# Heads of 64 dims issued in pairs, and a 64-row logit product padded to 128 rows

## The chip, the cores and the metric

The kernel runs on one core of one Trainium2 chip. The metric is the device time of one execution in microseconds (us). The engines are named as the profile names them: PE is the matrix engine (TensorE), PEld its weight loads, DVE is VectorE, ACT is ScalarE, POOL is GpSimd, and SP issues most of the DMAs. An "fp32r" operand is one that the kernel has rounded so that PE takes it in a single pass; a plain fp32 product is recorded as two passes, that is two matmul records and two weight loads.

## The reference

Two decoder layers (mixer and feed-forward network) and a third block work on 256 tokens of width 1024. Only the attention parts matter here. In short form:

```python
# layer 0, mixer "ab"
o_a = mla_attention(...)          # 8 heads: logits over 96 dims, values of 64 dims
o_b = swa_sink_attention(...)     # 8 heads of 64 dims, 2 key/value heads, a sink per head
# layer 1, mixer "cd"
o_c = forgetting_attention(...)   # 8 heads of 64 dims, decay from running sums of log-sigmoid gates
o_d = chunk_relpos_attention(...) # 8 heads of 64 dims, relative-position bias
# each of them, per head:
logits = q @ k.T * scale + bias   # causal or chunked mask
p = softmax(logits)
o = p @ v                         # 256 tokens x 64 dims
```

The mixers' outputs go through a projection, a residual and a layer norm, then through a SwiGLU network of width 2816. The third block has heads of 128 dims and is not touched by the change.

## The kernel before

Every weight matrix streams in once from one packed array, in blocks of at most 128 x 1032 numbers. A block lands in one of 5 "raw" buffers; ACT rounds it into a high part and DVE subtracts to get the low part (`block`). Both parts are tiles of the pool "h", which has `SLOTS` = 28 buffers and also holds q, k, v, attention outputs (`oT`), and the 11 tiles of the hidden layer (`hid`). The products of activations and weights are three fp32r passes (`gx`, `gw`).

All engine calls are recorded first, in program order, by the class `Order`. It then issues them by a list scheduler with modelled costs: each engine takes the earliest call in program order whose inputs are ready and whose buffer is free. A tile takes its buffer when the first call that touches it is issued. For some kinds of tile `RESERVE` lets a later tile go ahead of earlier ones as long as enough buffers stay free: for "h" a tile that goes ahead must find 4 free ones. Calls without inputs are ready from the start of the schedule; weight loads are paced by the 5 raw buffers, other DMAs by an added dependency (`AHEAD`). The engines then work through the issued order strictly one after the other.

Attention works head by head (`head`): two logit products (query tile 0 against key tile 0, 128 columns; query tile 1 against both, 256 columns) into a PSUM tile `a` of 4; DVE adds the bias and takes the row extreme (`tensor_tensor_reduce`); ACT takes the exponential with row sums; DVE normalises; PE transposes the three 128 x 128 blocks of probabilities; ACT copies them to a tile `pt` of 2; and two value products, plain fp32 with a stationary operand of 64 columns, write 64 of the 128 partitions of `po`. The second head of a pair writes the other 64. `hilo` then splits `po` for the output projection.

Three kinds of logit products occur. The sliding-window heads contract over 64 rows in plain fp32, the two heads of a pair in different halves of the rows. The latent-attention (MLA) heads contract over 96 rows. The "cd" heads use fp32r with the high and low parts of k stacked along the contraction: the first product takes 128 rows, the second one (q's low part `ql` with k's high part) takes 64 rows, in the half that k's high part occupies:

```python
own = slice(g * 64, g * 64 + 64)
self.head([(qq[:, g, i, :], kk[:, g, i, :]), (ql[own, i, :], kk[own, g, i, :])], bias, ...
```

Around the attention, `out_proj` multiplies by the output weights in units of two row tiles (4 "h" buffers each); the last 3 units (4 in the feed-forward network) are held until the end and used for token tile 0 and then for token tile 1, so that the layer norm of tile 0 runs beside the products of tile 1. `ffn` starts with the first 3 column groups (12 "h" buffers) for token tile 0.

Of the kernel before, what the change touches and what calls it, by code (L numbers as in the profile page):

```python
# [28 lines left out]
SLOTS = 28  # L29
# [12 lines left out]
class Order:  # L42
    """Takes the engine calls of the network in program order, and issues them in an order that a list
    scheduler finds: every engine takes the earliest call whose data and whose buffer are there."""
# [18 lines left out]
    def __init__(self, nc):  # L63
        self.ops, self.tiles, self.masks = [], {}, {}
        self.shift, self.pe = 0, []
# [70 lines left out]
    def add(self, eng, real, m, a, k):  # L136
# [3 lines left out]
        o = dict(i=len(self.ops), eng=eng, call=(real, m, a, k), deps=set(), tiles=set(), prio=len(self.ops) + self.shift)  # L140
# [21 lines left out]
        o["cost"] = self.cost(eng, m, a, k, ap_out + ap_in)  # L162
# [11 lines left out]
    def issue(self):  # L174
# [52 lines left out]
        while done < len(ops):  # L227
            for e in engs:
# [3 lines left out]
                while ready[e]:  # L232
# [20 lines left out]
                    if e == "ACT":  # L253
                        tab = self.TABLE.get(o["call"][2][2]) if o["call"][1] == "activation" else None
# [32 lines left out]
            if not ev:  # L287
                if done < len(ops):
                    raise RuntimeError("no call can go: " + str({e: [ops[i]["call"][1] for _, i in ready[e][:3]] for e in engs}))
                break  # L290
# [25 lines left out]
        for o in seq:  # L316
            real, m, a, k = o["call"]
            o["out"] = getattr(real, m)(*a, **k)  # L318


class Net:
    """Emits the whole network; `specs` lists the blocks of the packed weight stream in order."""

    def __init__(self, tc, ctx, a):
# [15 lines left out]
        self.ptp = pool("pt", 2)  # L340
# [9 lines left out]
    # ---- allocation helpers  # L350
# [37 lines left out]
    def w(self, name, li, rows, cols, pool=None):  # L388
        """rows: list of k-tiles (128 row indices each); returns per-k [(wh, wl)] APs of [128, len(cols)]."""
# [22 lines left out]
    def gw(self, out, x, w, c0, m=128):  # L412
        """out[cols, tok] = sum_k w_k[128k, cols].T @ x_k[128k, 256tok]"""
# [18 lines left out]
    # ---- activations held transposed  # L432
# [4 lines left out]
    def to_xT(self, src, t, xt):  # L437
        """src [128 tok, 1024] -> hi/lo parts of xT for token tile t; xt(i, half) gives [128, 4, 256]."""
# [9 lines left out]
    def bcast(self, name, n, off=0, tile_=None):  # L448
        """A row of n numbers on every partition."""
# [64 lines left out]
    def head(self, qk, bias, v, out, sign=-1.0, sink=None):  # L514
        """Causal blocks. qk: pairs [d, 256] whose products add up (q scaled, times sign); bias [128, 384] = t0k0 | t1k0 t1k1."""
        nc, V, mm = self.nc, self.nc.vector, self.nc.tensor.matmul
        s = self.pa()
        for i, (q, k) in enumerate(qk):
            mm(s[:, 0:128], q[:, 0:128], k[:, 0:128], start=i == 0, stop=i == len(qk) - 1)
        for i, (q, k) in enumerate(qk):  # L520
            mm(s[:, 128:384], q[:, 128:256], k, start=i == 0, stop=i == len(qk) - 1)
# [16 lines left out]
        pt = self.probs((L, L), exps, rs, nm, sign, [0, 128, 256], es)  # L538
        mm(out, v[0], pt[:, 0:256], start=True, stop=False)
        mm(out[:, 128:256], v[1], pt[:, 256:384], start=False, stop=True)  # L540
# [19 lines left out]
    # ---- the parts  # L560
# [34 lines left out]
    def rope(self, out, x, cos, sin):  # L595
        """x [128, heads, 32] (PSUM), cos / sin [128, heads, 32] with the scale folded in."""
# [9 lines left out]
    def norm_T(self, src, g, n, dst):  # L606
        """rms norm of PSUM src[t] ([128 tok, n]) with gain g, transposed hi/lo into dst [k] -> (hi, lo)."""
# [14 lines left out]
    def mixer_ab(self):  # L622
# [3 lines left out]
        # c_q | v_s  # L626
# [13 lines left out]
        # c_kv | k_r  # L640
# [15 lines left out]
        # k_s, q_s (pair j: heads j and 4 + j)  # L656
# [15 lines left out]
        # sliding-window attention  # L672
        o = []
        for j in range(4):
            if j % 2 == 0:
                oT = self.h([128, 2, 2, S], F32R)
            po = self.pa()
            for g in range(2):
                hh = 4 * g + j
                self.head([(qTs[g * 64:g * 64 + 64, j, :], kTs[g * 64:g * 64 + 64, :])], Bs[:, hh, :],  # L680
                          [vs[:, t, g * 64:g * 64 + 64] for t in range(2)], po[g * 64:g * 64 + 64, 0:256],
                          sink=(sk[:, 1, hh:hh + 1], sk[:, 0, hh:hh + 1]))
# [51 lines left out]
        for j in range(4):  # L734
            if j % 2 == 0:
                oT = self.h([128, 2, 2, S], F32R)
            po = self.pa()
            for g in range(2):
                hh = 2 * j + g
                self.head([(qTm[hh // 4][:, hh % 4, :], kTm[hh // 4][:, hh % 4, :])], mm_,  # L740
                          [vm[:, t, hh * 64:hh * 64 + 64] for t in range(2)], po[g * 64:g * 64 + 64, 0:256])
# [5 lines left out]
    def out_proj(self, name, li, o, krows, last_units, done, last_cols=(0, 512, 1024)):  # L747
        """o @ W; the last units go token tile by token tile, done(t, [(product, columns)]) after each."""
# [82 lines left out]
    def mixer_cd(self):  # L831
# [4 lines left out]
        # v_c | v_f | f in four groups of 258, token tile by token tile  # L836
# [10 lines left out]
        # log sigmoid of the forget gates, running sums, sums as rows  # L847
# [22 lines left out]
        def pair(cq, ck, scale, j):  # L870
            """q and k of heads 2j .. 2j + 3 with the high and low parts stacked along the contraction: per head
            k = [high; low], q = [high; high], and q's low part beside k's high one. Even heads have their high
            parts in the lower 64 partitions, odd heads in the upper."""
            qq, kk = self.h([128, 2, 2, S], F32R), self.h([128, 2, 2, S], F32R)
            ql = self.h([128, 2, S], F32R)
            lo, up = slice(0, 64), slice(64, 128)
            for c0, isq in ((cq, True), (ck, False)):
# [6 lines left out]
                for b, (own, other) in enumerate(((lo, up), (up, lo))):  # L884
# [3 lines left out]
                    V.scalar_tensor_tensor(ql[own] if isq else dst[other, b], pv[own], sc, dst[own, b].bitcast(F32),  # L888
# [3 lines left out]
        def heads(j, fox, v, qq, kk, ql):  # L892
            for i in range(2):
                oT = self.oT
                po = self.pa()
                for g in range(2):
                    hh = 2 * (j + i) + g
                    if fox:
                        pc = self.pa()
                        for t in range(2):  # L900
                            nc.tensor.transpose(pc[:, t * 128:(t + 1) * 128],
                                                cum[:, t, hh:hh + 1].to_broadcast([128, 128]), self.ident)
                        bias = self.lp([128, 384], F32, tag="L")
                        V.scalar_tensor_tensor(bias[:, 0:128], pc[:, 0:128], ncq[:, 0, hh:hh + 1], cm[:, 0:128],
                                               op0=OP.add, op1=OP.add)
                        V.scalar_tensor_tensor(bias[:, 128:384], pc[:, 0:256], ncq[:, 1, hh:hh + 1], cm[:, 128:384],
                                               op0=OP.add, op1=OP.add)
                    else:
                        bias = Bc[:, hh, :]
                    own = slice(g * 64, g * 64 + 64)  # L910
                    self.head([(qq[:, g, i, :], kk[:, g, i, :]), (ql[own, i, :], kk[own, g, i, :])], bias,
                              [v[:, t, hh * 64:hh * 64 + 64] for t in range(2)], po[g * 64:g * 64 + 64, 0:256],
                              sign=-1.0 if fox else 1.0)
# [11 lines left out]
    def mem_prep(self):  # L925
        """The memory comes transposed; its gain goes in with the split, its rms factor after the products."""
# [51 lines left out]
    def block2(self, mk, mv):  # L978
# [7 lines left out]
        # MOBA: groups of two heads (q q k k)  # L986
# [38 lines left out]
        def gated(po, c0, dst, hh):  # L1025
            """dst (hi, lo) <- po * 2 silu(gate)"""
# [23 lines left out]
        # memory attention  # L1050
# [19 lines left out]
        # gMLP  # L1070
# [39 lines left out]
        # gates and branches  # L1110
# [128 lines left out]
def layout(inputs):  # L1239
    """Everything but the weight stream, laid out for the chip."""  # L1240
# [59 lines left out]
```

## Time and profile before

| what | value |
|---|---|
| median of 3 runs | 952.17 us (951.37 to 955.55) |
| span of the profiled execution | 949.4 us |
| what lies around the span, against the median | 2.8 us |
| PE busy | 940.0 us (99%), 6504 matmuls |
| DVE busy | 602.0 us (63%) |
| ACT busy | 487.5 us (51%) |
| POOL busy | 23.9 us (3%) |
| DMA queue of the weights | 54.3% of 16 engines' span |
| mean granted clock of TensorE | 0.997 |

The span runs from the first to the last instruction. A busy share counts a matmul's pipeline until its end, so two matmuls that follow at 0.1 us may both last 0.28 us; what a matmul costs is better read from the start of one to the start of the next. The stages follow each other as: sliding-window and MLA attention from 39 to 92 us, output projection and layer norm to 130, the feed-forward network to about 298, the projections of mixer "cd" to 335, its attention to 421, output projection and layer norm to 451, the second network to about 630, and the third block to the end.

### The profile page before, as it was taken

To read this page: it belongs to the slowest core of one execution; us is meant where nothing else is said; L and a number is where in the kernel's file an instruction comes from. 1 tells how busy PE (TensorE), PEld (TensorE's weight loads), DVE (VectorE), ACT (ScalarE), POOL (GpSimd) and SP (SyncE) were. 2 spreads that over 40 slices of the span, in tenths; PEclk is the share of its full clock that TensorE was granted. 3 is DMA by queue.
4 is the path that set the end of the run, shared out by engine and by line. 5 is a ranking of instruction groups with operands and counts; after the bars stand their busy time and mean duration, and the time that the engine had idled before them with its cause. 6 is when DMAs were issued, how large, how long until landed. Compare 5 with 4: busy or idle time off the path is not lost.

```text
span 949.4 us, 16237 instructions
## 1 busy us (share of the span) xinstructions
PE 940.0 (99%) x6504; PEld 857.2 (90%) x6504; DVE 602.0 (63%) x1064; ACT 487.5 (51%) x839; POOL 23.9 (3%) x32
## 2 busy tenths in 40 slices
PE   8999999999999999999999999999999999999997
PEld 7977899999889988879999998898889999999996
DVE  5777984545548556779545465495448697565553
ACT  6677474444424757546443455254446574445441
POOL 0100100000001000000000000000000000000000
PEclk9999999999999999999999999999999999999999
DMA  9732595556664714345655768266544545665631
GB/s 324 279 138 80 172 328 166 172 162 216 221 207 171 251 60 129 138 133 172 213 172 155 222 234 295 70 197 222 178 155 141 182 161 189 189 189 179 193 118 45
DMA packets 50155, 171.30 MB, mean 180 GB/s; under 512 B 5920, under 2 KB 7456, under 8 KB 49824
## 3 DMA queue, kind: packets, MB, share of 16 engines
q1 hardware_dynamic: 49792, 169.74, 54.3%
q8 instruction: 51, 0.84, 0.3%
q10 hardware_dynamic: 288, 0.52, 0.1%
q14 instruction: 24, 0.20, 0.1%
HBM read 169.19 MB, written 1.05 MB: 179 GB/s over the span
## 4 chain that ended last, share of the span: by engine, by line
PE 96%; DVE 1%; DMA 1%; ACT 1%; POOL 0%; issue 0%; SPq 0%; POOLq 0%; ACTq 0%
PE g L318 85%; PE a L318 10%; DVE h L318 1%; DMA raw<-in_wstream_dram 1%; DMA h<-in_wstream_dram 1%; POOL s L318 0%; ACT h L318 0%; DVE res L318 0%; SPq L318 0%; DVE s L318 0%; DVE xT L318 0%; ACT y L318 0%; POOLq L1294 0%; ACT xT L318 0%; ACT pt L318 0%
## 5 line engine op out<-in xcount | busy, mean ns | idle before, releaser
L318 PE MATMUL g<-h,h 128*128 128x256 f32 (+2 forms) x2520 | 438.2, 330 | 0.0
L318 DVE TENSOR_TENSOR h<-raw,h 128x1024 fp32r<-128x1024 f32 (+4 forms) x300 | 349.4, 1184 | 127.8 <-PE g L318 51.9
L318 PEld LDWEIGHTS g<-h,h 128*128 128x128 f32 x2520 | 371.3, 188 | 44.9 <-issue 1.9
L318 ACT ACTIVATE h<-raw 128x1024 fp32r<-128x1024 f32 (+4 forms) x300 | 301.0, 1025 | 123.1 <-PE g L318 71.0
L318 PE MATMUL g<-xT,h 128*128 128x256 f32 x2424 | 297.7, 283 | 0.0
L318 PEld LDWEIGHTS g<-xT,h 128*128 128x128 f32 x2424 | 291.1, 189 | 2.1 <-issue 1.2
L318 PE MATMUL g<-h,xT 128*128 128x256 f32 (+3 forms) x744 | 111.8, 310 | 1.5 <-ACT xT L318 1.4
L318 PEld LDWEIGHTS g<-h,xT 128*128 128x128 f32 x744 | 101.3, 189 | 10.9 <-ACT xT L318 2.7
L318 ACT ACTIVATE si<-g 128x256 f32<-128x256 f32 x68 | 26.2, 385 | 119.7 <-PE g L318 118.9
L318 ACT ACTIVATE h<-g 64x512 fp32r<-64x512 f32 (+11 forms) x67 | 31.4, 476 | 53.1 <-PE g L318 41.0
L318 DVE TENSOR_TENSOR si<-si,g 128x256 f32<-128x256 f32 x50 | 21.0, 419 | 58.1 <-ACT si L318 58.1
L318 ACT ACTIVATE L<-L,s 128x128 f32<-128x128 f32 (+1 forms) x84 | 37.7, 451 | 15.0 <-DVE s L318 14.8
L318 POOL TENSOR_TENSOR s<-s,mhalf 128x1 f32<-128x1 f32 x18 | 20.0, 1111 | 762.1 <-DVE s L318 762.0
L318 PE MATMUL a<-pt,h 128*64 128x128 f32 (+3 forms) x168 | 34.9, 331 | 0.2 <-ACT pt L318 0.2
L318 ACT ACTIVATE pt<-a 128x384 f32<-128x384 f32 (+1 forms) x42 | 21.1, 501 | 26.0 <-PE a L318 25.7
L318 DVE TENSOR_TENSOR h<-si,h 128x256 fp32r<-128x256 f32 x48 | 20.3, 423 | 19.7 <-ACT h L318 19.6
L318 PE MATMUL a<-h,h 128*128 128x256 f32 (+5 forms) x152 | 32.6, 331 | 0.1
L318 PEld LDWEIGHTS a<-pt,h 128*64 128x64 f32 (+1 forms) x168 | 21.1, 148 | 12.3 <-issue 3.2
L318 PEld LDWEIGHTS a<-h,h 64*128 64x128 f32 (+2 forms) x152 | 22.7, 187 | 7.5 <-issue 1.5
L318 ACT ACTIVATE h<-a 128x256 fp32r<-128x256 f32 (+5 forms) x41 | 18.5, 478 | 18.6 <-PE a L318 18.2
L318 PE MATMUL a<-ident,L 128*128 128x128 f32 (+1 forms) x132 | 27.0, 280 | 0.0
L318 DVE TENSOR_SCALAR L<-L,s 128x128 f32<-128x128 f32 (+1 forms) x84 | 23.4, 320 | 1.2
(107 smaller groups left out, 430.3 us busy)
## 6 DMA issues: line engine op xcount, KB each, us to landing
raw<-in_wstream_dram SPq DMA_DIRECT2D x262, 512.0 KB, 4.3
raw<-in_wstream_dram SPq DMA_DIRECT2D x16, 384.0 KB, 3.2
raw<-in_wstream_dram SPq DMA_DIRECT2D x8, 516.0 KB, 4.4
raw<-in_wstream_dram SPq DMA_DIRECT2D x10, 256.0 KB, 2.9
gb<-in_ln_g_dram SPq DMA_DIRECT2D x4, 512.0 KB, 6.9
gb<-in_ln_b_dram SPq DMA_DIRECT2D x4, 512.0 KB, 7.4
h<-in_wstream_dram SPq DMA_DIRECT2D x3, 512.0 KB, 6.3
B<-in_swa_bias_dram SPq DMA_DIRECT2D x1, 1536.0 KB, 7.3
```

The source lines that it names most:

```text
L318: o["out"] = getattr(real, m)(*a, **k)
```

## The change

1. `head` is cut into three parts: `logits`, `soft` (bias, softmax, transposes) and `values`. A new `head_pair` takes two heads: logits of both, softmax of both, then the four value products of both alternating between the two heads. `Order` gets a `bundle`: several PE calls become one unit of the schedule with one cost, so that nothing is put between them.
2. For the sliding-window heads (`rows=True`) the four logit products of a pair are a bundle too.
3. In mixer "cd", `ql` becomes a [128, 2, 2, S] tile with a zero half for each head, filled by two memsets on POOL per tile (8 in all), and the second logit product takes all 128 rows.
4. The pool `pt` goes from 2 to 4 tiles and `SLOTS` from 28 to 27. Docstrings and comments go.

```diff
-SLOTS = 28
+SLOTS = 27
...
+    @contextmanager
+    def bundle(self, cost):
+        self.one = (cost, [])
+        yield
+        self.one = None
...
-        o = dict(i=len(self.ops), eng=eng, call=(real, m, a, k), deps=set(), tiles=set(), prio=len(self.ops) + self.shift)
+        if self.one and self.one[1]:
+            o = self.one[1][0]
+            assert o["eng"] == eng == "PE"
+            o["calls"].append((real, m, a, k))
+        else:
+            o = dict(i=len(self.ops), eng=eng, calls=[(real, m, a, k)], deps=set(), tiles=set(),
+                     prio=len(self.ops) + self.shift)
...
-        self.ptp = pool("pt", 2)
+        self.ptp = pool("pt", 4)
...
+    def values(self, pt, v, out):
+        return [(out, v[0], pt[:, 0:256], True, False), (out[:, 128:256], v[1], pt[:, 256:384], False, True)]
...
+    def head_pair(self, qk, bias, v, sign=-1.0, sink=(None, None), rows=False):
+        s = [self.pa(), self.pa()]
+        c = [self.logits(qk[g], s[g]) for g in range(2)]
+        if rows:
+            with self.nc.bundle(1000.0):
+                self.mms([x for ab in zip(*c) for x in ab])
+        else:
+            self.mms(c[0])
+            self.mms(c[1])
+        pt = [self.soft(s[g], bias(g), sign, sink[g]) for g in range(2)]
+        po = self.pa()
+        c = [self.values(pt[g], v[g], po[g * 64:g * 64 + 64, 0:256]) for g in range(2)]
+        with self.nc.bundle(1030.0):
+            self.mms([x for ab in zip(*c) for x in ab])
+        return po
...
-            ql = self.h([128, 2, S], F32R)
+            ql = self.h([128, 2, 2, S], F32R)
             lo, up = slice(0, 64), slice(64, 128)
+            nc.gpsimd.memset(ql[up, 0].bitcast(F32), 0.0)
+            nc.gpsimd.memset(ql[lo, 1].bitcast(F32), 0.0)
...
-                    V.scalar_tensor_tensor(ql[own] if isq else dst[other, b], pv[own], sc, dst[own, b].bitcast(F32),
+                    V.scalar_tensor_tensor(ql[own, b] if isq else dst[other, b], pv[own], sc, dst[own, b].bitcast(F32),
...
-                    self.head([(qq[:, g, i, :], kk[:, g, i, :]), (ql[own, i, :], kk[own, g, i, :])], bias,
+                po = self.head_pair([[(qq[:, g, i, :], kk[:, g, i, :]), (ql[:, g, i, :], kk[:, g, i, :])]
+                                     for g in range(2)], bias,
```

## Rows read from the trace of the kernel before

**Rows 1.** The page: busy time by engine, and the shares of the last chain
```profile
PE 940.0 (99%) x6504; PEld 857.2 (90%) x6504; DVE 602.0 (63%) x1064; ACT 487.5 (51%) x839; POOL 23.9 (3%) x32
...
PE 96%; DVE 1%; DMA 1%; ACT 1%; POOL 0%; issue 0%; SPq 0%; POOLq 0%; ACTq 0%
```

**Rows 2.** Groups of PE instructions by form: busy us, mean ns, idle before
```profile
L318 PE MATMUL a<-pt,h 128*64 128x256 f32 x64 | 20.0, 405 | 0.2 <-ACT pt L318 0.2
...
L318 PE MATMUL a<-h,h 64*128 64x128 f32 x32 | 7.4, 316 | 0.0
```

**Rows 3.** Chain in order of time: start, us, what; a long run of products
```profile
453.69 105.26 PE g L318 x891
```

**Rows 4.** Timeline of PE near 347 us: start, us, engine, instruction, count
```profile
346.76 0.84 PE L318 MATMUL g<-xT,h 128*128 128x256 f32 x5
347.53 0.86 PE L318 MATMUL a<-pt,h 128*64 128x256 f32 x4
348.32 0.55 PE L318 MATMUL a<-ident,L 128*128 128x128 f32 x3
```

**Rows 5.** Timeline of PE and of its weight loads near 89 us
```profile
89.45 0.88 PE L318 MATMUL a<-pt,h 128*64 128x256 f32 x8
90.26 0.96 PE L318 MATMUL g<-h,h 128*128 128x512 f32 x3
...
89.45 0.64 PEld L318 LDWEIGHTS a<-pt,h 128*64 128x64 f32 x8 [0.37 <-ACT pt L318]
```

**Rows 6.** Timeline of PE near 335 us: the first four "cd" heads' logits
```profile
335.24 4.61 PE L318 MATMUL a<-h,h 128*128 128x128 f32 x16
```

**Rows 7.** Stretches: length, busy of PE, PEld, DVE, ACT, POOL; PEclk, DMA share, GB/s
```profile
335.24:339.78 4.54, 4.54 (x18) 2.95 (x16) 3.01 (x16) 2.29 (x8) 0.00 (x0) 1.00 0.45 143
339.78:343.22 3.44, 3.44 (x17) 3.44 (x17) 2.05 (x11) 0.60 (x4) 0.00 (x0) 0.50 0.00 0
```

**Rows 8.** Timeline of PE, 40 to 57 us: sliding-window logits and what follows
```profile
40.92 1.57 PE L318 MATMUL a<-h,h 64*128 64x128 f32 x12
42.43 0.71 PE L318 MATMUL g<-h,h 128*128 128x480 f32 x2
...
53.82 0.92 PE L318 MATMUL a<-h,h 64*128 64x128 f32 x6
54.67 0.87 PE L318 MATMUL a<-pt,h 128*64 128x256 f32 x4
...
55.94 0.70 PE L318 MATMUL a<-h,h 64*128 64x256 f32 x2
56.57 0.92 PE L318 MATMUL g<-h,h 128*128 128x288 f32 x5
```

**Rows 9.** Stretches by stage, columns as in Rows 7
```profile
39.00:70.00 31.00, 30.85 (x192) 23.27 (x191) 24.98 (x93) 23.33 (x69) 0.00 (x0) 1.00 0.52 187
70.00:92.00 22.00, 22.00 (x125) 16.03 (x124) 14.50 (x64) 17.20 (x52) 0.00 (x0) 1.00 0.23 73
92.00:130.00 38.00, 37.72 (x257) 34.57 (x256) 34.20 (x42) 22.20 (x28) 2.98 (x2) 1.00 0.66 221
...
335.00:421.00 86.00, 85.94 (x517) 68.83 (x516) 57.53 (x173) 51.90 (x123) 0.00 (x0) 0.98 0.34 111
421.00:451.00 30.00, 30.00 (x212) 27.87 (x212) 26.10 (x34) 15.57 (x20) 2.91 (x2) 1.00 0.48 160
```

**Rows 10.** Timeline of POOL: a memset and the call that follows it
```profile
0.83 0.26 POOL L318 MEMSET L<- 128x192 f32 x1
19.14 1.18 POOL L318 TENSOR_TENSOR s<-s,mhalf 128x1 f32<-128x1 f32 x2 [18.05 <-DVE s L318]
```

**Rows 11.** Groups of DVE, 335 to 451 us, and ACT, 39 to 92 us: weight splits
```profile
L318 DVE TENSOR_TENSOR h<-raw,h 128x1024 fp32r<-128x1024 f32 x27 | 32.3, 1219 | 2.4 <-ACT h L318 2.3
...
L318 ACT ACTIVATE h<-raw 128x1024 fp32r<-128x1024 f32 x9 | 9.4, 1051 | 0.0
```

**Rows 12.** Chain in order of time between the first mixer and its network
```profile
120.08 5.85 DMA raw<-in_wstream_dram
```

More of the change, by code (lines that the diff above doesn't have):

```diff
@@ L2 @@
 import heapq
-from contextlib import ExitStack
+from contextlib import ExitStack, contextmanager
 import numpy as np
@@ L161, in add @@
         o["deps"].discard(o["i"])
-        o["cost"] = self.cost(eng, m, a, k, ap_out + ap_in)
+        if self.one:
+            if self.one[1]:
+                return
+            self.one[1].append(o)
+        o["cost"] = self.one[0] if self.one else self.cost(eng, m, a, k, ap_out + ap_in)
         if eng == "PE":
@@ L253, in issue @@
                     if e == "ACT":
[L254 removed]
+                        _, m, a, _ = o["calls"][0]
+                        tab = self.TABLE.get(a[2]) if m == "activation" else None
                         if tab and tab != table:
@@ L288, in issue @@
                 if done < len(ops):
-                    raise RuntimeError("no call can go: " + str({e: [ops[i]["call"][1] for _, i in ready[e][:3]] for e in engs}))
+                    raise RuntimeError("no call can go: " + str({e: [ops[i]["calls"][0][1] for _, i in ready[e][:3]] for e in engs}))
                 break
@@ L316, in issue @@
         for o in seq:
-            real, m, a, k = o["call"]
-            o["out"] = getattr(real, m)(*a, **k)
+            for real, m, a, k in o["calls"]:
+                getattr(real, m)(*a, **k)
 class Net:
@@ L512, in probs, with logits, mms, soft @@
         return pt
[L514 to L521, printed above, removed]
+    def logits(self, qk, s):
+        n = len(qk) - 1
+        return ([(s[:, 0:128], q[:, 0:128], k[:, 0:128], i == 0, i == n) for i, (q, k) in enumerate(qk)]
+                + [(s[:, 128:384], q[:, 128:256], k, i == 0, i == n) for i, (q, k) in enumerate(qk)])
+    def mms(self, calls):
+        for out, l, r, first, last in calls:
+            self.nc.tensor.matmul(out, l, r, start=first, stop=last)
+    def soft(self, s, bias, sign=-1.0, sink=None):
+        nc, V = self.nc, self.nc.vector
         L = self.lp([128, 512], F32, tag="L")
@@ L676, in mixer_ab @@
                 oT = self.h([128, 2, 2, S], F32R)
[L677 to L682, printed above, removed]
+            G = [slice(0, 64), slice(64, 128)]
+            po = self.head_pair([[(qTs[r, j, :], kTs[r, :])] for r in G], lambda g: Bs[:, 4 * g + j, :],
+                                [[vs[:, t, r] for t in range(2)] for r in G],
+                                sink=[(sk[:, 1, hh:hh + 1], sk[:, 0, hh:hh + 1]) for hh in (j, 4 + j)], rows=True)
             self.hilo(oT[:, 0, j % 2, :], oT[:, 1, j % 2, :], po[:, 0:256])
@@ L736, in mixer_ab @@
                 oT = self.h([128, 2, 2, S], F32R)
[L737 to L741, printed above, removed]
+            hs = (2 * j, 2 * j + 1)
+            po = self.head_pair([[(qTm[hh // 4][:, hh % 4, :], kTm[hh // 4][:, hh % 4, :])] for hh in hs],
+                                lambda g: mm_, [[vm[:, t, hh * 64:hh * 64 + 64] for t in range(2)] for hh in hs])
             self.hilo(oT[:, 0, j % 2, :], oT[:, 1, j % 2, :], po[:, 0:256])
@@ L894, in heads, with bias @@
                 oT = self.oT
-                po = self.pa()
-                for g in range(2):
+                def bias(g):
                     hh = 2 * (j + i) + g
[L898 to L910, printed above, removed]
-                    self.head([(qq[:, g, i, :], kk[:, g, i, :]), (ql[own, i, :], kk[own, g, i, :])], bias,
-                              [v[:, t, hh * 64:hh * 64 + 64] for t in range(2)], po[g * 64:g * 64 + 64, 0:256],
-                              sign=-1.0 if fox else 1.0)
@@ new lines, in bias @@
+                    if not fox:
+                        return Bc[:, hh, :]
+                    pc = self.pa()
+                    for t in range(2):
+                        nc.tensor.transpose(pc[:, t * 128:(t + 1) * 128],
+                                            cum[:, t, hh:hh + 1].to_broadcast([128, 128]), self.ident)
+                    b = self.lp([128, 384], F32, tag="L")
+                    V.scalar_tensor_tensor(b[:, 0:128], pc[:, 0:128], ncq[:, 0, hh:hh + 1], cm[:, 0:128],
+                                           op0=OP.add, op1=OP.add)
@@ new lines, in bias @@
+                    V.scalar_tensor_tensor(b[:, 128:384], pc[:, 0:256], ncq[:, 1, hh:hh + 1], cm[:, 128:384],
+                                           op0=OP.add, op1=OP.add)
+                    return b
+                po = self.head_pair([[(qq[:, g, i, :], kk[:, g, i, :]), (ql[:, g, i, :], kk[:, g, i, :])]
+                                     for g in range(2)], bias,
+                                    [[v[:, t, c:c + 64] for t in range(2)]
+                                     for c in (128 * (j + i), 128 * (j + i) + 64)], sign=-1.0 if fox else 1.0)
```

10 lines of the change are left out of this document (6 added, 4 removed).

## The prediction

> **What bounds the kernel now.** I read the page first: busy times and the chain that ended last [rows 1]. PE is busy for 940.0 of 949.4 us and the chain lies on PE for 96% of it, so time taken from PE is time taken from the kernel, as long as nothing else comes last in its place. But a busy PE is not an efficient one. The measure of a good stretch is the second network: 891 products in 105.26 us, 0.118 us from one to the next [rows 3]. In the attention stages I therefore read start to start. The groups by form give the counts: 64 passes of 256 columns with a 64-column stationary operand are two per head, so 32 heads, 16 pairs; 32 logit records of 64x128 are 16 of the sliding-window heads (two passes each of 8 heads) and 16 of the "cd" heads (one each of 16) [rows 2].
>
> **Value products (part 1 of the change).** One head's four passes take 347.53 to 348.32, 0.79 us [rows 4]. The 5 fp32r products between two such blocks take 346.76 to 347.53, 0.77 us, where 5 x 0.118 = 0.59 would do: 0.18 us go at the changes from 128 to 64 columns and back. A head costs 0.79 + 0.18 = 0.97 us, a pair 1.94. What the pair costs side by side stands in the same trace, once: the last two MLA heads happened to fall together, and their 8 passes last 89.45 to 90.26, 0.81 us, with 8 weight loads in 0.64 us [rows 5]. So 0.81 + 0.18 = 0.99 for a pair, 0.95 saved. One of the 16 pairs has it already: 15 x 0.95 = 14.3 us. The bounds: if nothing overlapped, only one change of columns per pair would go, 15 x 0.18 = 2.7 us; at most 15 us.
>
> Here a rule of the Trainium skill speaks against the change. The page "TensorE: Matmul & The Clock Gate" (Part 3, The mechanism) says that weight loads overlap running matmuls only where the row groups differ, and two 64-column operands over the same 128 rows share theirs. By that rule the pairs would give the 2.7 us instead of the 14.3. This trace does not agree: the 8 loads of the one accidental pair fit into 0.64 us.
>
> **"cd" logits (part 3).** The first four heads' 16 products run alone in 335.24 to 339.78, that is 4.54 us, 1.14 per head [rows 6, 7]; every second one has 64 rows, so each of the four per head pays a change of shape. With 128 rows throughout they are an ordinary fp32r stream: 4 x 0.118 = 0.47 us or a little less, since two have only 128 columns. I take 0.46; the bounds of the new price are 0.35 (128-column products at half the price) and 0.47. Saved: 16 x (1.14 - 0.46) = 10.9 us (10.7 to 12.6).
>
> **Clock.** Right behind those 16 products the granted clock is 0.50, the lower of its two levels, for 3.44 us; 16 or 17 products run in it [rows 7] where 16 x 0.118 = 1.9 would do: 1.5 us lost. The stretch in front shrinks to 1.8 us, and I expect the drop to go: 1.5 us (0 to 1.5).
>
> **Sliding-window logits (part 2).** Twelve passes, three heads, take 40.92 to 42.43, 1.51 us, and a second run like it 1.50; two more heads fall apart, 0.85 and 0.63 us [rows 8]. Sum 4.5 us for 8 heads. A head costs 0.50 in the runs and 0.74 in the split ones, so something overlaps in the runs already. If that is one pair, and the third head costs what the four value passes of the same columns do, 0.79 [rows 4], a pair is 0.72; I take 0.85, since the changes of shape then come once for two heads and not for three: 4 x 0.85 = 3.4, saved 1.1 us (0 to 1.6).
>
> Sum taken from PE: 14.3 + 10.9 + 1.5 + 1.1 = 27.8 us.
>
> **What comes back.** Three things can become late when PE isn't.
> - DVE and ACT in the first mixer. From 39 to 70 us DVE works 24.98 of 31 us; PE would lose 4 pairs x 0.95 + 1.1 = 4.9 us there, so DVE would fill 24.98 of 26.1, 96%. The fullest DVE stretch in the table is 34.20 of 38, 90% [rows 9]; at 90% the stretch can't go below 27.8 and 1.7 us of the gain are lost. From 70 to 92 ACT works 17.20 of 22, and PE would lose 3 x 0.95 = 2.9: ACT at 90%. At its present 78% all 2.9 would be lost. So 0 to 4.6 us; I take 2.5, since output products wait there as filler, but their weights have to be split by the same two engines.
> - DVE in the second mixer: 57.53 of 86 us would become 57.53 of about 66 (8 pairs, 10.9 and 1.5 off), 87%, as full as it is from 421 to 451 already (26.10 of 30) [rows 9]. Loss 0 if 87% holds, 6 us if 80% is the limit; I take 2.
> - The "h" buffers. `SLOTS` falls by one, and there is a second, hidden cut: the new memsets have no inputs, so POOL can issue them at the start of the schedule. The memset of a tile L, which has none either, ran at 0.83 us, 18 us before POOL's next call [rows 10]. With `RESERVE` asking for 4 free buffers, the four `ql` tiles would be taken at once and held until mixer "cd" has used them: 23 buffers for the first third of the kernel, not 27. The memsets themselves are free: 192 columns took 0.26 us, so 512 are some 0.7, 8 x 0.7 = 5.6 us by about 7 us, and POOL's next call is at 19 us. What the cut costs: at the end of the first output projection 12 buffers hold weights and 4 hold outputs; before, 12 were left, the whole start of the network; now 7. Five buffers are 2.5 blocks, each 1.22 us of DVE and 1.05 us of ACT [rows 11], moved into a stretch where DVE is at 90% [rows 9] and the chain goes through a raw load of 5.85 us [rows 12]: 0 to 3.1 us. The same at the end of the network (16 held, 4 hidden tiles: 3 left in place of 8): 0 to 3.1. I take 2.5 for both.
>
> The larger `pt` pool and the shorter hold of `po` (taken only at the bundle) cost nothing; the cover is that PSUM tiles `a` are freed by DVE and ACT, which are late less often than PE now. A bundle waits for the later of two `pt` tiles, and everything behind it on PE with it; weight products stand in between as they do now, and where that cover is missing the wait is part of the 4.6 and the 6 us above.
>
> Sum: 27.8 - 2.5 - 2 - 2.5 = 20.8 us. The profiled execution becomes 949.4 - 20.8 = 928.6, and with the 2.8 us that the median lies above it, 931.4 us.
>
> **The rivals.**
> - All of it lands: PE has filler everywhere, and the planner, whose modelled 1030 for a pair stands against the 0.99 us measured, orders better. 952.2 - 27.8 = 924.4 us (919 to 927). For it: today no engine makes PE wait. Against it: DVE at 96% from 39 to 70. Chance 0.23.
> - More comes back: DVE, ACT and buffers at their upper bounds, 4.6 + 6 + 6.2 = 16.8: 952.2 - 27.8 + 16.8 = 941.2 us. Chance 0.13.
> - The pairs don't overlap (the change doesn't do what it says): 2.7 + 10.9 + 1.5 + 1.1 = 16.2, less some 4 back: 940 us. The overlapped pair speaks against it [rows 5]. Chance 0.04. This is where the rule of the Trainium skill above would end.
> - Slower: the first network starves. One of its blocks is used up in 24 x 0.118 = 2.8 us and takes 1.05 + 1.22 = 2.3 us and the signals to refill once its two buffers are free. With 11 hidden tiles 17 buffers are left before and 12 after, 6 blocks. It decides below 4 blocks (two in use, two in refill): then PE waits about 2.3 us per column group, 22 x 2.3 = 51 us against the 20.8 won: 982 us. Six blocks are enough by this count, so chance 0.08.
> - No visible change, gains eaten by a rearranged order: 0.06.
>
> **How the numbers follow.** The forecast case, 927 to 939 us, has 0.46. A measurement of this kernel can tell about 0.5% from no change, here 947.4 and 956.9. Faster: 0.46 + 0.23 + 0.13 + 0.04 = 0.86; same 0.06; slower 0.08. The range reaches from the first rival to the end of the second and third, 920 to 947: it leaves out the last two cases and a little at the lower end, together under 0.2. The predicted time is that of the likeliest case, 931 us.
>
> **What would show it.** After: 8 passes of the value products per pair in about 0.81 us, 16 times; "cd" logits at 0.12 us from start to start and no record with 64 rows there; no clock of 0.50 near 340 us; the second mixer's attention some 18 us shorter, the first mixer's 5; POOL memsets on "h" at 1 to 7 us; the stretch from 92 to 130 us as long as before or a little longer, with DVE still at 90%. Wrong would be PE waits for ACT or DVE in the attention stages that add up to over 10 us, or gaps in the run of the first network.

## The result and the profile after

The changed kernel takes 930.75 us (median of 4 runs, 929.24 to 931.08), the kernel before 951.77 beside it (950.0 to 955.55): a ratio of 0.9757, 95% interval 0.9727 to 0.9786. It is faster by 21.0 us; 20.8 were forecast. The two profiled executions differ by 949.4 - 927.5 = 21.9 us, and the stages below are those of the profiled executions. The profiled execution of the changed kernel is the fastest of its four, with a mean granted clock of 0.999 where the other three have 0.996 to 0.997, so differences of 1 to 2 us between medians are better read from the profiles.

The page of the changed kernel, busy times by engine and shares of the last chain, answers to [rows 1]:

```profile
PE 916.5 (99%) x6504; PEld 846.4 (91%) x6504; DVE 600.4 (65%) x1064; ACT 484.1 (52%) x839; POOL 29.1 (3%) x40
...
PE 95%; ACT 2%; DVE 2%; DMA 1%; issue 0%; SPq 0%; POOL 0%; POOLq 0%; ACTq 0%
```

The same 6504 matmuls, 23.5 us less busy time on PE, and a chain that is still PE's. To cut the span into stages I use POOL's inverse square roots, which both kernels compute at the same places: the last one of the first mixer's norms, the first one of the layer norm behind the first mixer, the second one of the layer norm behind the first network, and the first one behind mixer "cd". POOL's timeline, kernel before and then the changed kernel (start, us, instruction):

```profile
27.56 1.39 POOL L318 TENSOR_TENSOR s<-s,mhalf 128x1 f32<-128x1 f32 x1 [2.76 <-DVE s L318]
101.19 1.52 POOL L318 TENSOR_TENSOR s<-s,mhalf 128x1 f32<-128x1 f32 x1 [72.24 <-DVE s L318]
299.38 1.46 POOL L318 TENSOR_TENSOR s<-s,mhalf 128x1 f32<-128x1 f32 x1 [10.66 <-DVE s L318]
426.01 1.46 POOL L318 TENSOR_TENSOR s<-s,mhalf 128x1 f32<-128x1 f32 x1 [125.18 <-DVE s L318]
```

```profile
27.04 1.39 POOL L336 TENSOR_TENSOR s<-s,mhalf 128x1 f32<-128x1 f32 x1 [2.73 <-DVE s L336]
95.30 1.52 POOL L336 TENSOR_TENSOR s<-s,mhalf 128x1 f32<-128x1 f32 x1 [66.86 <-DVE s L336]
293.00 1.45 POOL L336 TENSOR_TENSOR s<-s,mhalf 128x1 f32<-128x1 f32 x1 [10.66 <-DVE s L336]
402.47 1.45 POOL L336 TENSOR_TENSOR s<-s,mhalf 128x1 f32<-128x1 f32 x1 [108.01 <-DVE s L336]
```

The first mixer's stretch goes from 73.6 to 68.3 us, the network with its two norms from 198.2 to 197.7, mixer "cd" from 126.6 to 109.5. From there to the end it is 523.4 before and 525.0 after. The same four marks, read in the profile of every kernel of this study, give a table (difference to the kernel before, us):

| kernel | median of its runs | to the first mark | first mixer | first network | mixer "cd" | rest |
|---|---|---|---|---|---|---|
| before | 951.77 | 27.6 | 73.6 | 198.2 | 126.6 | 523.4 |
| changed | 930.75 | -0.5 | -5.4 | -0.5 | -17.2 | +1.6 |
| value pairs alone | 940.58 | +0.2 | -7.0 | -0.3 | -5.2 | +0.8 |
| padding alone | 940.02 | -1.0 | -0.1 | +0.2 | -11.8 | +0.7 |
| changed, one head after the other | 930.23 | +0.5 | -5.3 | -0.5 | -17.1 | +1.6 |
| changed, late memsets | 928.61 | -0.3 | -5.0 | -0.1 | -17.5 | +0.2 |
| changed, no unit of logits | 927.62 | 0.0 | -7.0 | -0.6 | -17.1 | +1.1 |
| the last two together | 928.78 | +0.5 | -6.9 | -0.3 | -17.6 | +1.5 |
| changed, no unit, 28 buffers | 929.02 | 0.0 | -7.0 | -0.1 | -16.4 | +1.4 |
| changed, unscaled | 927.40 | +0.3 | -7.5 | -0.5 | -17.1 | +1.1 |
| changed, no row sums | 927.30 | +0.2 | -6.7 | -0.2 | -18.2 | +1.4 |
| changed, split copies | 936.76 | +1.7 | -2.4 | -0.5 | -13.3 | +0.7 |
| changed, same half | 941.39 | -0.2 | +0.6 | -0.5 | -10.8 | +0.7 |
| before, unscaled | 954.99 | +0.5 | +2.2 | -0.2 | +0.3 | +0.6 |

The medians come from five groups of runs, in which the kernel before had 951.76 to 952.83. Every row of the rest holds +0.2 to +1.6, whatever was changed ahead of it, so a difference of that size can't be put down to one edit.

What a stage loses to waits shows, at the least, in PE's idle time: the stage's length less PE's busy time. The lines give the first mixer before, changed, and changed without the unit of logits, then mixer "cd" before and changed (columns as in [rows 7]):

```profile
27.56:101.19 73.63, 73.34 (x446) 57.86 (x446) 56.12 (x178) 53.76 (x135) 1.39 (x1) 1.00 0.49 163
27.04:95.30 68.26, 66.36 (x446) 54.25 (x446) 56.95 (x179) 50.70 (x133) 1.40 (x2) 1.00 0.56 197
27.59:94.21 66.62, 66.05 (x446) 54.67 (x446) 56.80 (x179) 50.46 (x133) 1.39 (x2) 1.00 0.59 200
...
299.38:426.01 126.63, 126.57 (x838) 108.48 (x837) 84.80 (x207) 76.41 (x161) 1.46 (x1) 0.99 0.47 159
293.00:402.47 109.47, 108.50 (x836) 99.68 (x835) 87.22 (x210) 77.51 (x163) 1.46 (x2) 1.00 0.58 197
```

PE is idle for 0.3 us of the first mixer before, for 1.9 in the changed kernel and for 0.6 without the unit; in mixer "cd" for 0.1 and 1.0. The prediction put its limit for such waits at 10 us.

How a pair looks now. PE's timeline and its weight loads in mixer "cd", to be read against [rows 4, 5]:

```profile
337.03 0.87 PE L336 MATMUL a<-pt,h 128*64 128x256 f32 x8
337.83 0.86 PE L336 MATMUL g<-xT,h 128*128 128x256 f32 x5
...
337.02 0.63 PEld L336 LDWEIGHTS a<-pt,h 128*64 128x64 f32 x8
```

From 337.03 to 337.83: 8 passes in 0.80 us. Eleven of the 16 pairs last 0.80 us until the next product. The other five have a wait inside or right behind them and last 0.91 to 2.19 us; three of these five, with the two longest (1.48 and 2.19), are pairs of sliding-window heads, the other two (1.03 and 1.16) of "cd" heads. The two longest:

```profile
53.12 0.87 PE L336 MATMUL a<-pt,h 128*64 128x256 f32 x8
55.31 0.55 PE L336 MATMUL a<-ident,L 128*128 128x128 f32 x3 [1.32 <-ACT h L336]
56.21 0.55 PE L336 MATMUL a<-ident,L 128*128 128x128 f32 x3 [0.36 <-DVE h L336]
56.69 1.55 PE L336 MATMUL a<-pt,h 128*64 128x256 f32 x8
58.17 0.86 PE L336 MATMUL g<-h,h 128*128 128x256 f32 x5
```

Behind the pair at 53.12 nothing starts on PE until 55.31, and the pair at 56.69 takes 1.48 us until the next product. Here PE waits for ACT and DVE; in the kernel before, its waits in this stage came to 0.2 us in all [rows 2]. Two stretches of the changed kernel show how full these two engines are where PE waits and where it doesn't (columns as in [rows 7]):

```profile
39.00:58.00 19.00, 17.24 (x125) 12.71 (x123) 16.39 (x66) 15.73 (x50) 0.00 (x0) 1.00 0.77 292
...
70.00:86.00 16.00, 16.00 (x105) 12.09 (x104) 13.71 (x59) 15.29 (x47) 0.00 (x0) 1.00 0.26 88
```

From 39 to 58 us PE is idle for 1.76 us, with DVE busy for 86% and ACT for 83%; from 70 to 86 us ACT is busy for 96%, and PE is never idle.

The logits of the first four "cd" heads, which took 4.54 us [rows 6]:

```profile
328.80 2.33 PE L336 MATMUL a<-h,h 128*128 128x128 f32 x16
330.96 1.23 PE L336 MATMUL g<-xT,h 128*128 128x256 f32 x9
...
331.00:350.00 19.00, 18.64 (x158) 17.52 (x157) 15.24 (x53) 15.06 (x41) 0.00 (x0) 1.00 0.37 119
```

2.16 us, and the stretch behind them, the last line, has a granted clock of 1.00: in this execution the drop of [rows 7] is gone.

Last, the memsets, in POOL's timeline, where [rows 10] has nothing between 0.83 and 19.14 us:

```profile
1.14 4.53 POOL L336 MEMSET h<- 64x512 f32 x8
```

All eight run at the start of the kernel, as read from the code: the four `ql` tiles are held from there on.

### The profile page after: what moved, and what is told of

Read it like the earlier page. It is cut to its first block, busy times and chain, and to the rows that moved or that the text cites. A ratio compares the mean times of both kernels' runs of the same rounds, so it can differ in the third digit from the quotient of the medians.

```text
span 927.5 us, 16281 instructions
## 1 busy us (share of the span) xinstructions
PE 916.5 (99%) x6504; PEld 846.4 (91%) x6504; DVE 600.4 (65%) x1064; ACT 484.1 (52%) x839; POOL 29.1 (3%) x40
## 4 chain that ended last, share of the span: by engine, by line
PE 95%; ACT 2%; DVE 2%; DMA 1%; issue 0%; SPq 0%; POOL 0%; POOLq 0%; ACTq 0%
PE g L336 87%; PE a L336 8%; ACT h L336 1%; DVE h L336 1%; DMA h<-in_wstream_dram 1%; DVE L L336 0%; ACT L L336 0%; SPq L336 0%; ACT pt L336 0%; POOL s L336 0%; DVE s L336 0%; ACT y L336 0%; POOLq L1340 0%; ACT xT L336 0%; DVE res L336 0%
## 5 line engine op out<-in xcount | busy, mean ns | idle before, releaser
L336 ACT ACTIVATE h<-si 128x256 fp32r<-128x256 f32 x48 | 19.7, 410 | 12.1 <-DVE si L336 12.0
L336 ACT ACTIVATE h<-a 128x256 fp32r<-128x256 f32 (+5 forms) x41 | 18.3, 474 | 14.7 <-PE a L336 14.3
L336 DVE SCALAR_TENSOR_TENSOR res<-res,g 128x512 f32<-128x512 f32 x16 | 10.9, 683 | 20.5 <-PE g L336 20.5
L336 DVE TENSOR_SCALAR L<-L,s 128x128 f32<-128x128 f32 (+1 forms) x84 | 23.4, 321 | 1.1
L336 PE MATMUL a<-h,h 128*128 128x256 f32 (+5 forms) x152 | 23.0, 307 | 1.0 <-DVE h L336 0.7
L336 PE MATMUL a<-pt,h 128*64 128x256 f32 (+3 forms) x168 | 23.2, 332 | 0.0
```

## The experiments

**The two parts alone.** First the value pairs without padding and without the unit of the sliding-window logits (a `...` inside a line marks what is left out of it):

```diff
-... for hh in (j, 4 + j)], rows=True)
+... for hh in (j, 4 + j)])
...
-            ql = self.h([128, 2, 2, S], F32R)
-            nc.gpsimd.memset(ql[up, 0].bitcast(F32), 0.0)
-            nc.gpsimd.memset(ql[lo, 1].bitcast(F32), 0.0)
+            ql = self.h([128, 2, S], F32R)
...
-... (ql[:, g, i, :], kk[:, g, i, :]) ...
+... (ql[g * 64:g * 64 + 64, i, :], kk[g * 64:g * 64 + 64, g, i, :]) ...
```

> The value products go in pairs as one unit (SLOTS 27, four pt tiles); the logit products are as before: the second one of the cd heads has 64 rows, no memsets, and the sliding-window logits are no unit. My theory: 15 pairs x 0.95 = 14.3 us come off PE, and 2 to 3 us of it are given back in the first mixer, so 939 to 941 us, with the clock drop near 340 us still there. Rival (what PE gives up is mostly lost to waits for DVE and ACT): 945 us or more. If this run and the next one together win clearly more than the whole change does, the two parts share a limit.

940.58 us, ratio 0.9859 (0.9816 to 0.9903). As forecast in total. The surprise is in the first mixer: 7.0 us shorter, where the whole change has only 5.4. The clock drop is there, and now twice, each time at the end of a run of 16 logit products of which every second has 64 rows: from 0.4 us behind the end of the first run, and from 0.8 us ahead of the end of the second. The second run in PE's timeline, and the stretches of the two drops (columns as in [rows 7]):

```profile
349.55 4.89 PE L336 MATMUL a<-h,h 128*128 128x128 f32 x16 [0.36 <-DVE h L336]
354.37 3.10 PE L336 MATMUL g<-xT,h 128*128 128x256 f32 x14
...
333.12:336.56 3.44, 3.44 (x19) 3.44 (x18) 3.37 (x15) 1.12 (x6) 0.00 (x0) 0.50 0.19 49
353.60:357.04 3.44, 3.44 (x14) 3.00 (x15) 3.33 (x18) 1.64 (x8) 0.00 (x0) 0.50 0.01 5
```

Then the padding without the pairs, in the kernel before:

```diff
-            ql = self.h([128, 2, S], F32R)
+            ql = self.h([128, 2, 2, S], F32R)
+            nc.gpsimd.memset(ql[up, 0].bitcast(F32), 0.0)
+            nc.gpsimd.memset(ql[lo, 1].bitcast(F32), 0.0)
...
-... (ql[own, i, :], kk[own, g, i, :]) ...
+... (ql[:, g, i, :], kk[:, g, i, :]) ...
```

> The kernel before with only the second logit product of the cd heads over 128 rows (the wider ql and its memsets; heads one by one, SLOTS 28). My theory: 10.9 us of logits and 1.5 us of clock come off PE, 1 to 2 us come back: 940 to 942 us, no granted clock of 0.50 near 340 us. Rival (the 64-row products hide behind other work): within 2 us of the kernel before, 950 to 954 us. If the clock drop stays although the logits are short, the stretch of 64-row products was not what led to it.

940.02 us, ratio 0.9847 (0.9811 to 0.9884): all of it, 11.8 us, in mixer "cd". The 16 products there take 2.04 us, from 334.24 to the next product at 336.28, and no clock drop follows. In mixer "cd" the two parts add up: 5.2 + 11.8 = 17.0, the whole change has 17.2. Over the whole span they win more than the change does, 11.4 + 12.0 = 23.4 us in the profiles against 21.9; that is the first mixer, where the value pairs alone gain 1.6 us more than the whole change, so the two parts needn't share a limit.

```profile
334.24 2.20 PE L318 MATMUL a<-h,h 128*128 128x128 f32 x16
336.28 4.07 PE L318 MATMUL g<-xT,h 128*128 128x256 f32 x33
```

**What makes a pair cheap.** Is it the alternating order, the two column halves, or only that the shape changes once per pair? Two edits tell. The order first:

```diff
         with self.nc.bundle(1030.0):
-            self.mms([x for ab in zip(*c) for x in ab])
+            self.mms(c[0] + c[1])
```

> The changed kernel, but inside a pair's unit the value products of the first head come before those of the second, not alternating. Theory A: PE runs products of different column halves side by side whenever they stand near each other in its queue, whatever their order: a pair's 8 passes stay at about 0.81 us, the time within 2 us of the changed kernel's 930.8. Theory B: only neighbours overlap, so the order is what makes the pair: a pair costs between 0.81 and 1.59 us, about 1.3, and the time is 16 x 0.5 = 8 us longer, 938 to 939 us.

930.23 us, ratio 0.9746 (0.9709 to 0.9782). A pair whose second head is issued whole behind the first, in PE's timeline:

```profile
63.11 0.88 PE L336 MATMUL a<-pt,h 128*64 128x256 f32 x8
63.92 1.32 PE L336 MATMUL g<-h,h 128*128 128x256 f32 x6
```

0.81 us against 0.80. The alternating order is worth nothing; it is enough that the two heads stand next to each other. That also explains why the one accidental pair of the kernel before had the full effect [rows 5]. Then the halves, with the order of the last run; the copies of `po` change at all three places that make them:

```diff
-c = [self.values(pt[g], v[g], po[g * 64:g * 64 + 64, 0:256]) for g in range(2)]
+c = [self.values(pt[g], v[g], po[0:64, g * 256:g * 256 + 256]) for g in range(2)]
...
-self.mms([x for ab in zip(*c) for x in ab])
+self.mms(c[0] + c[1])
...
-self.hilo(oT[:, 0, i, :], oT[:, 1, i, :], po[:, 0:256])
+for g in range(2):
+    r = slice(g * 64, g * 64 + 64)
+    self.hilo(oT[r, 0, i, :], oT[r, 1, i, :], po[0:64, g * 256:g * 256 + 256])
```

> The changed kernel, but both heads of a pair write their value products to the same 64 partitions of po (the second head beside the first in the free dimension), first head before second, as one unit; the copies of po are then two of 64 partitions each. Theory A (the gain is that products of different column halves run at once): the 8 passes of a pair follow each other and take about 4 x 0.216 + 4 x 0.109 = 1.3 us and the change of shape, not 0.81; 16 x 0.5 to 0.65 = 8 to 10 us slower than the run with split copies alone. Theory B (the gain is that the shape changes once per pair and not once per head): the same as that run within 2 us.

941.39 us, ratio 0.9896 (0.9867 to 0.9924). A pair in PE's timeline and its weight loads:

```profile
78.27 1.51 PE L336 MATMUL a<-pt,h 128*64 128x256 f32 x8
79.72 0.77 PE L336 MATMUL a<-ident,L 128*128 128x128 f32 x5
...
78.27 1.27 PEld L336 LDWEIGHTS a<-pt,h 128*64 128x64 f32 x8 [0.29 <-DVE s L336]
```

1.45 us, in 14 of the 16 pairs. So running side by side is worth 1.45 - 0.80 = 0.65 us per pair. The other 0.30 us of the prediction's 0.95 come with the two heads standing next to each other: their passes take 1.45 us and not 2 x 0.79, and one visit to another shape, 0.18 us by the prediction's estimate, falls away. The copies of `po` had to be split for this kernel; the control does that alone, with `po[r, 0:256]` as their source:

> The changed kernel with each copy of po as two of 64 partitions, as in the run where both heads write the same half, but with the value products as in the change. It prices the split copies: 16 more copies of 0.38 us on ACT and of 0.42 us on DVE. If PE still sets the time, within 1.5 us of the changed kernel's 930.8; if ACT or DVE does in the attention stages, up to 6 us more.

936.76 us, ratio 0.9839 (0.9815 to 0.9863). The control is 6.0 us slower than the changed kernel, though PE has the same work: 3.0 us are lost in the first mixer, 3.9 in mixer "cd", by the table, 3.7 of these 6.9 as idle time of PE. So PE no longer sets the time of these stages alone. That also covers part of the lost overlap: the kernel with both heads in one half is 4.6 us slower than its control, not the 8 to 10 expected. In the two stages PE's busy time is some 8 us longer than the control's, and its idle time 2.8 us shorter. The price of a pair is shown by its rows; in the time of the kernel only part of it shows.

**Who waits now.** Two kernels take work from DVE, one from ACT. The scaling of the probabilities goes first, in the changed kernel and in the one before:

```diff
-            nc.vector.tensor_scalar(L[:, c0:c1], L[:, c0:c1], ri[:, t:t + 1], None, op0=OP.mult)
+            pass
```

> The changed kernel without the two products per head on DVE that scale the probabilities by the inverse row sum (left out of the result, in the heads of 64 and of 128 dims): 0.63 us of DVE less per head, some 10 us in mixer cd. Theory (DVE and ACT took back 2 to 3 us of mixer cd's gain): 2 to 4 us faster than the changed kernel, 927 to 929 us, the gain in mixer cd and in the first mixer. Rival (the waits are not theirs; the rest is changes of shape and order): the same within 1 us.

> The kernel before without the same scaling on DVE (left out of the result). Before, PE alone set the time: within 1 us of the kernel before, 951 to 954 us. If it gains as much as the changed kernel does from this, DVE was already in the way before the change and the theory that it takes part of the gain falls.

The changed kernel goes to 927.40 us (ratio 0.9738, 0.9723 to 0.9753), 2.1 us of it in the first mixer and nothing in mixer "cd". The kernel before goes to 954.99 (ratio 1.0039, 1.0019 to 1.0059): with less work it is slower by 0.4%, 2.2 us of it in the first mixer. A gain or loss of 2 us could thus be the order of the calls, and the idle time of PE tells the two apart. In the kernel before, unscaled, PE is busy for 2.3 us more of the first mixer and idle for no longer than with the scaling: order, and no wait. In the changed kernel PE's idle time there falls from 1.9 to 0.6 us: DVE's work is in the way in the first mixer now. In mixer "cd" PE's idle time doesn't fall without the scaling (1.9 us against 1.0), so nothing shows that DVE's work costs anything there. Then ACT's row sums:

```diff
-            nc.scalar.activation(L[:, c0:c1], src[:, c0:c1], AF.Exp, bias=nm[:, t:t + 1], scale=sign,
-                                 accum_out=rs[:, t:t + 1])
+            nc.scalar.activation(L[:, c0:c1], src[:, c0:c1], AF.Exp, bias=nm[:, t:t + 1], scale=sign)
...
-            nc.vector.tensor_tensor(rs, rs, es, op=OP.add)
+            nc.vector.tensor_tensor(rs, nm, es, op=OP.add)
+        else:
+            rs = nm
```

> The changed kernel without the row sums that ACT collects with each exponential (left out of the result; the inverse is taken of the row extremes, which are there anyway): two accumulator reads of 0.19 us less per head on ACT, some 6 us in mixer cd. Adding copies to ACT and DVE cost 6 us, taking work from DVE alone gained 2 us in the first mixer and nothing in mixer cd. Theory (ACT and the chain through it is what PE waits for in the attention stages now): 2 to 5 us faster than the changed kernel, 926 to 929 us, over 1 us of it in mixer cd, whose stage then is over 18 us shorter than before. Rival (the rest in mixer cd is nobody's wait but the price of the products themselves): mixer cd within 0.5 us of the changed kernel's, 17.2 us shorter than before.

927.30 us, ratio 0.9738 (0.9717 to 0.9759). Mixer "cd" is 18.2 us shorter than before, 1.1 more than in the changed kernel, and PE's idle time there falls from 1.0 to 0.4 us, so part of what is missing there hangs on ACT. The inverse of the sums also no longer waits for the exponentials, so this doesn't separate ACT's time from the length of the chain through it. The chain itself agrees. By line, for mixer "cd" in the kernel before and in the changed one:

```profile
by line: PE g L318 57.6%; PE a L318 42.8%; issue 0.1%
```

```profile
by line: PE g L336 42.6%; PE a L336 23.7%; ACT h L336 13.7%; DVE h L336 7.8%; DVE L L336 3.7%; issue 3.4%; ACT L L336 2.8%; ACT pt L336 2.1%; DVE s L336 0.4%; ACTq L336 0.0%
```

Before, the chain never left PE there; after, some 30% of it runs over ACT and DVE, most of that over the tiles `h` (the split of weights, q and k). PE goes on with other products meanwhile: of the 109.5 us it is idle for 1.0.

**The unit of the sliding-window logits.** It is the one part that can be taken out by a single argument (`rows=True`):

> The changed kernel without the unit of the sliding-window logits; all else as in it. With pairs of values alone the first mixer was shorter by 6.98 us, with the whole change by 5.38. Theory: the unit of the logits is what loses it (it holds PE and two PSUM tiles until both heads can go, and DVE and ACT then are late): this kernel is about 1.6 us faster than the changed one, 929.2 us, and its first mixer some 7 us shorter than before. Rival (the prediction's: the unit saves 1.1 us, and the loss is DVE's and ACT's limit or the early memsets): 931 to 932 us.

927.62 us, ratio 0.974 (0.9725 to 0.9756), and the first mixer 7.0 us shorter than before, as with the value pairs alone. The interval of the ratio overlaps that of the whole change, but all four runs (927.46 to 927.89) lie below all of the changed kernel's (929.24 to 931.08), and three kernels without the unit agree on 6.9 to 7.0 us in the first mixer while three with it (changed, one head after the other, late memsets) have 5.0 to 5.4. PE's idle time in the first mixer divides them in the same way: 0.1 to 0.6 us without the unit, the value pairs alone among them, and 1.8 to 1.9 with it. The unit does what it says: in the changed kernel a pair's logits take 0.86 us,

```profile
40.38 0.93 PE L336 MATMUL a<-h,h 64*128 64x128 f32 x8
41.24 1.58 PE L336 MATMUL g<-h,h 128*128 128x480 f32 x6
```

4 x 0.86 = 3.4 us in place of the 4.5 of [rows 8]. But as a unit the third and fourth pair come at 47.60 and 52.26 us:

```profile
47.60 0.93 PE L336 MATMUL a<-h,h 64*128 64x128 f32 x8
...
52.26 0.93 PE L336 MATMUL a<-h,h 64*128 64x128 f32 x8
```

Without the unit six of the eight heads have their logits by 44.55, and the last two happen to fall together:

```profile
40.91 1.57 PE L336 MATMUL a<-h,h 64*128 64x128 f32 x12
42.41 0.70 PE L336 MATMUL g<-h,h 128*128 128x480 f32 x2
43.05 1.57 PE L336 MATMUL a<-h,h 64*128 64x128 f32 x12
44.55 1.36 PE L336 MATMUL g<-h,h 128*128 128x480 f32 x5
...
51.41 0.93 PE L336 MATMUL a<-h,h 64*128 64x128 f32 x8
52.27 0.87 PE L336 MATMUL a<-pt,h 128*64 128x256 f32 x8
```

That is 1.50 + 1.50 + 0.86 = 3.9 us, so in this kernel the unit itself saves PE only 0.4 us. With it the softmax of the later heads starts later, and PE waits for it between 53 and 58 us. The kernel without the unit is the fastest of this study among those that leave nothing out.

**The h buffers.** The memsets get the dependency that late DMAs have:

```diff
+        if m == "memset" and "h" in [self.tiles[x]["tag"] for x in o["tiles"]]:
+            j = bisect.bisect(self.pe, (self.pe[-1][0] - self.AHEAD, 0))
+            o["deps"].add(self.pe[max(j, FIRST) - 1][1])
```

> The changed kernel, but each memset of ql is given the added dependency that late DMAs have, so that it takes its h buffer some 16 us of planned PE work before its own place and not at the start of the kernel. If the early taking costs what the prediction put down for the h buffers, 1 to 3 us come back: 928 to 930 us, in the stretches between the first mixer and its network and between the network and mixer cd. Rival (buffers are not short in the first third): the same within 1 us, 930 to 932 us.

> The changed kernel without the unit of the sliding-window logits and with the memsets of ql late. If both gains are real and add up, 1.6 + 2.1 us: 927 us. If the late memsets bring nothing of their own, 929 us, as the run without the unit alone.

The first of the new memsets runs at 295.60 us instead of 1.14. The kernel takes 928.61 us (ratio 0.973, 0.9694 to 0.9767), by the medians 2.1 us less than the changed one, by the profiles 0.6. But the first mixer and the network, where the buffers are free again, are 0.4 us longer each than with the early memsets, and together with the removed unit the late memsets make the kernel slower, 928.78 against 927.62. That early taking costs anything is not shown. The other way round, 28 buffers and two `pt` tiles instead of 27 and four, without the unit:

> The changed kernel without the unit of the sliding-window logits, with two pt tiles and 28 h buffers as before (four pt tiles and 27 in the change). Stages behind mixer cd are together 0.9 to 1.6 us longer with the change than before. If the one buffer less is the reason, they are as before and this kernel is about 1 us faster than the run without the unit alone (927.6): 926.6 us. If four pt tiles matter to the pairs, it is slower, 929 us or more, with the loss in the attention stages. Rival: no difference, 927 to 928 us.

929.02 us, ratio 0.9763 (0.9741 to 0.9784): 0.7 us are lost in mixer "cd" and 0.5 in the first network, and the rest is no shorter than with 27. PE's idle time in mixer "cd" is 1.5 us against 1.0, so most of the 0.7 us is a wait; whether it is one for the `pt` tiles is open at this size.

## Why the prediction was right, step by step

- *Value products, 14.3 us.* The price of a pair was read from one accidental pair as 0.81 us and is 0.80. The gain with this part alone is 7.0 + 5.2 = 12.2 us, with one clock drop more than before in it; by the drop's 1.5 us it would be 13.7. The bound "nothing overlaps" is refuted by the 0.80 us and by the 1.45 us of the kernel with both heads in one half.
- *"cd" logits, 10.9, and the clock, 1.5.* Together 12.4; the padding alone took 11.8 from mixer "cd". Four heads cost 2.04 to 2.16 us, 0.51 to 0.54 each where 0.46 was put down: the products among themselves are not quite the dense stream. The drop of the clock went with the stretch in front of it, in the profiles of all kernels with padding.
- *Sliding-window logits, 1.1.* The term was right for PE (4.5 to 3.4 us) and wrong for the kernel. The sum took a gain on PE for a gain in time and put the wait that the unit brings nowhere. Taking the unit out gains 1.6 us in the first mixer, 1.3 of them idle time of PE.
- *What comes back in the first mixer, 2.5.* The predicted gain there was 7 x 0.95 + 1.1 = 7.8, the measured one is 5.4: 2.4 came back. The size was right and the reason half: DVE and ACT are waited for (PE's idle time falls by 1.3 us without the scaling, and by as much without the row sums), but not because they are full at 96%. PE waits where they are busy for 86% and 83%, and not where ACT is at 96%. Without the unit the same DVE and ACT work lets the stage be 7.0 us shorter. That the size came out is luck.
- *What comes back in mixer "cd", 2.* Expected off PE were 7.6 + 10.9 + 1.5 = 20.0, measured are 17.2, so 2.8 came back. The step named DVE, and nothing bears that out: less work on DVE gained nothing there. Of the 2.8 us, 0.8 to 1.3 are the logits at 0.51 to 0.54, an estimate from the first groups of four heads, and 0.9 are idle time of PE that wasn't there before. Without ACT's row sums 1.1 us return, 0.6 of them idle time. The remainder is open.
- *The h buffers, 2.5.* The mechanism was read rightly from the code, eight memsets at 1.14 us, and its price was wrong: the stretch from the first mixer's end through the network is 0.5 us shorter, not longer. This term is the clearest miss of the sum; the table has no stage in which the buffers were missed.
- *Not foreseen:* 1.6 us behind mixer "cd". All kernels of the study have 0.2 to 1.6 us of it, with 28 buffers too, so it isn't the smaller pool alone. Its cause is open.

So the mechanisms of the two large terms were right, and that the total came out within a microsecond is partly luck, because errors met: 3.0 us too much for the buffers (2.5 put down, 0.5 gained) against 1.6 us behind mixer "cd" and 0.8 more inside it. The rivals: "all of it lands" (924.4) is the nearest, and the kernel without the unit comes within 3.2 us of it; "more comes back" (941.2) would need some 10 us more to come back than did; non-overlapping pairs and a starving network are refuted by the 0.80 us and by a network as long as before. The rule of the Trainium skill, as the prediction read it ("TensorE: Matmul & The Clock Gate", Part 3, The mechanism), does not hold here: over the same 128 rows the weight loads run beside the passes even where both heads use one half, 1.27 us of loads within the pair's 1.45, and where the halves differ 8 loads take 0.63 us.

## What to carry to other kernels

Read a tuned kernel's PE time start to start and by shape: a busy share of 99% hid about 0.18 us at each visit to another operand shape, passes that could run side by side, and a clock drop behind a run of shape changes. Put products that use different halves of the columns next to each other (0.65 us per pair here by overlap), and try padding short contractions whose neighbours have 128 rows (11.8 us for 16 heads here, with the clock drop). But a unit holds its first calls back until the inputs of its last one are there: the unit of the sliding-window logits saved PE 0.4 us and made its stage 1.6 us longer. To tell a wait from a costlier order, compare PE's idle and busy time in the stage.

## What the runs showed of the hardware

Products of different column halves run side by side even where, in the queue, all passes of the first head stand ahead of those of the second: 0.81 us against 0.80 for the alternating order, and 1.45 us where both heads use the same half. The granted clock fell to 0.50, the lower level, for 3.44 us at the end of a run of 16 logit products with alternating row counts, once in the kernel before and twice with the value pairs alone. PE was busy throughout each run; 0.36 us of idle time stood ahead of one of the three runs. In the profiles it never fell behind 16 padded products.
